# Attention products for two heads at once in a hybrid decoder layer, with a new order of the first stage

## The chip, the cores and the metric

One core of one Trainium2 chip. The metric is device time in microseconds (us) of one execution, the median of several runs. The kernel computes in float32; large products are made of three matmuls on halves of the numbers (below). Names: PE is the matmul engine TensorE, DVE VectorE, ACT ScalarE, POOL GpSimd, SP the engine that issues the DMAs.

## The reference

One decoder layer over 512 tokens of width 1024: native sparse attention (8 heads of 64, two groups of four heads that share keys and values) and a gated DeltaNet (4 heads of 128) in parallel, merged by gates, a layer norm, then a gated MLP with a short convolution (width 2816) and a second layer norm. What matters here:

```
# attention: three branches, each head's result weighted by a gate
p = jax.nn.softmax(s, axis=-1)              # s: scores of a branch, masked, with ALiBi
o = g[0] * o_cmp + g[1] * o_slc + g[2] * o_win      # o_x = p_x @ v_x
...
def conv_ffn(x, w_up, conv_w, w_down):
    h = causal_dwconv(x @ w_up, conv_w)     # width 3
    gate, val = jnp.split(h, 2, axis=-1)
    return (jax.nn.silu(gate) * val) @ w_down
```

With 512 tokens and 8 blocks of 64, the top 8 blocks are all blocks, so the selected branch and the window branch are causal attention over the whole sequence, with keys of their own.

## The kernel before

Every float32 matrix is split into a rounded part and the rest (names ending in h and l, or hi and lo; type F32R), and a product is hi·hi + hi·lo + lo·hi: three matmuls. ACT makes the hi part, DVE (sometimes POOL) the lo part. For weights these are the tiles `wh`, `wl` (`dh`, `dl` in the down-projection), from a tile `raw` that a DMA brings.

**First stage** (up to about 324 us): input projections (`gemm_t`, PSUM tile `pg`), the DeltaNet (`gdn_...`, PSUM `pd`) and the attention (PSUM `pa` for scores and transposes, `po` for results). Its steps are recorded by name and engine, then issued in the order that two tables give: `DRAWN`, the order of the steps, and `GIVEN`, the order of single instructions (`t0P*3` is three PE instructions of step t0, `@k` picks the k-th). `PLACE` says which buffer of a ring each new tile takes, `ENGINE` which engine does an operation that could run on several.

Attention of a head h has six units (`UNITS`): u = 0 to 3 are the token blocks 2 and 3 of each of the two large branches, u = 4 and 5 the blocks 0 and 1 of both branches at once. `scores(h, u)` makes scores and softmax weights in a `big` tile; `flip(h, u, s)`, issued one unit later (LAG), transposes them with PE into `pa`, from where ACT writes the hi part (`pth`) and DVE the lo part (`ptl`). After every second unit PE multiplies by the values (`vcat`, whose 128 columns hold hi and lo of the values): for u = 1, 3 the later 256 tokens, four key blocks; for u = 5 the earlier 256, two key blocks of two branches. Each key block takes a matmul with `pth` and one with `ptl`, 256 columns wide, all into one bank `po`. The compressed branch (`vcb` with `pc`) adds two matmuls 512 wide and closes the head; then `ob` copies the lower half of `po` and DVE adds both halves into `oT`. `po` has one buffer.

**Middle**: merge of the two mixers (PSUM `px`, `pm`), output projection (`pw`), layer norm. Here and later a scheduler orders the instructions by priority in the order of the code.

**FFN**: 22 tiles p, each a gate and a value half (b = 0, 1; PSUM `pu`): product, three convolution taps (ACT, then DVE twice, into `fa`), tanh and two products (`fth`, the last one on POOL). The down-projection is one level of Strassen-like sums over pairs of tiles: `halves` splits activations 11, 12, 22 and the sum s2 into hi and lo; s1, s3, s4 are kept in `SUM` and split later; `weight_sums` makes the sums of weights (`traw`) and sends them to `tdn`. Seven products (`mul`) follow, into PSUM `pdna` and `pdnb`; `add` adds a finished bank to `x1`, `work` holds generators that give out one piece of other work after every two weight tiles.

Of the kernel before, what the change touches and what calls it, by code (L numbers as in the profile page):

```python
# [18 lines left out]
S = 512  # L19
# [50 lines left out]
def layout(a):  # L70
# [18 lines left out]
    for i in range(8):  # L89
# [35 lines left out]
DRAWN = "q0 k0 i0 q1 j0 m0 c n0 i1 v0 j1 p0 v1 a0 o0 b0 y0 a1 b1 m1 n1 i2 j2 a2 b2 o1 y1 m2 v2 q2 a3 n2 b3 o2 y2 q3 p1 g0 k1 a4 i3 j3 b4 g1 m3 a5 n3 b5 a6 v3 g2 o3 b6 g3 a7 g4 b7 y3 g5 g6".split()  # L125
GIVEN = """
t0S@2 t0S@1 t0V@2 t0A@1 t0P@6 t0V@3 t0P@7 t0V@1 t0P@8 t0P@9 t0P@10 t0S t0A t0P@3 t0P@4 t0P@11 t0V t0P*3 t0S*2 t0V*2
t0A t0V t0P t0P@15 t0P@16 t0P@21 t0P*4 t2S t2A t0P@22 t0P@23 t2S t2A t0P*3 t2P@6 t2V*2 t2S t2A@3 t2A t2V t2P@3 t2P@9
t2P t2P@10 t2P@11 t2P*6 t2P@18 t2P@15 t2P@21 t2P@19 t2P@22 t2P*2 t2V t2P t2P@20 t2P@23 t2P*2 t4S@1 t4A@2 t4V@2 t4S
t4A@1 t4V@1 t4A t4P@9 t4P@10 t4V t4P t4P@3 t4P*2 t4S t4A t4P@11 t4P@6 t4P@7 t4P@21 t4P@8 t4P@22 t4P t4P@12 t4P@13 t4V  # L130
t4P@18 t4P t4P@15 t4P@16 t4P@17 t4P@19 t4P@20 t4P*2 t6S t6A t6S*2 t6A@2 t6A t6P@9 t6P@3 t6P@6 t6P t6V@2 t6V@1 t6P@10
t6P@7 t6V t6A t6P@4 t6P t6P@11 t6V t6P@8 t6P@18 t6P@5 t6P@19 t6P@20 t6P*5 t6P@21 t6P*4 w20S uA@8 w20A w20V w20A uA@2
uA@11 cV@8 cV@10 uA@5 w20V zS@6 dV@2 q0P*12 dV@3 dA*2 dV@4 dV@5 dV@6 dV@7 dV@8 dV@9 dV@1 dV@10 dV@11 q0P*12 w18S
w18A@1 w18V@1 uA@6 uV@2 zS@2 w21S w18A w18V k0P*15 dV@12 dV@13 dV@14 dV@15 k0P*2 uA@4 uA@7 uA@3 uA w0S q0A@2 q0A*2
dV@16 k0P*4 dV@17 dV@18 w0A zV@1 k0P q0V@2 q0V@1 q0V k0P w16S w0A w0V@1 w0V k0P k0V*4 dV@19 cS@1 i0P*13 zS@5 w21A w21V
dV@20 k0A*2 w1S uA@9 cV i0P*4 w1G i0P*3 s01P k0V*2 s01P i0P*3 s00P i0P q1P w21A q1P*12 s00P uV w1V i0V*2 dV@21 dV@22
w21V i0V zS s01V s01A q1P*8 uV@3 q1P*3 uA@10 zS i0V i0A zV w17S w1G dV@23 w1V dV@24 uV s04P*2 q1A uA j0P uV dA j0P*3
dV@25 dV@26 dV@27 dV j0P*12 w16A q1A@2 w16G q1A q1V@1 q1V@2 w16A w16G j0P*5 w4S j0P*3 q1V j0A w17A m0G j0V cP*19 i0G
cP m0P j0V*2 cS@3 m1V m0G m0P m0A cS i0G cP*4 dP w17V i0P dP i0P w4V w4V@2 dP i0P w4V*2 cA dA i0P j0A j0V i0A cS i0A
# [24 lines left out]
s21V n1V q2P*2 n1V*3 s25P v2A n1P w23V w23G n1P*3 n1A n1P y0V*2 n1P*3 n1V f21P y0P*3 s23A f21P y0P f21P n1P*3 s25V n1P
y0V s25A q2P s30P q2P*3 s30P n1V s23V v2V s24V f21P w22V s23V s30V f21A n1P*4 n1A n1P n1V n1P*7 n1A n1V q2P*3 n1P*6
f21V n1P*2 s23A q2P*2 n1A n1V q2P n1P@38 n1P@39 n1P@40 n1P@41 n1P*4 n1A@7 n1A f23P w23V s25V s25A v2V*2 f20P f23P*2
w23G m3G f20P f15V n1P*3 n2G@1 n1P n1A q2P*2 s25V s25V@4 q2P o1P o1A f22P f20P m2P*4 m2A o1P q3P*2 q2P o1V o1P@3 o1V@2
s25V f20A i2P*2 f22P f23P i2P*2 f20V f22P j2V i2A@6 i2A@7 i2A i2A@8 o1P@4 o1A q3P q2P q3P*2 o1P@6 o1V@3 i2A@9 i2A*3
i2V i2G q3P*3 o1P@8 w24S o1V@5 s30A m2P q2P*2 o1P@9 i2V*2 m2V m2P m2V@2 m2V q3P*7 w11S f22A q3P f22V s30V j1V j1G s30V
f23A m2P w11A f23V o1A@3 q2A q2A@2 q2A*2 q2V@1 q2V w11V s33P o1P@11 o1V@6 m2P m2V q3P n2V m1G w11A w11V f21P*2 s30A  # L170
f21P*6 s35P*2 n2V*2 q3P*7 q3A@2 q3V@1 q3A@1 w24V@1 s35V s35A s31P*2 s31V i2V@8 q3A@3 y2P*6 w12S y2P q3A y2P*5 f23P*4
w24V f23P y2P*7 m2V s35V s35A w24G@1 o1P@13 f25P*4 o1V@8 f24P*2 q3V w24G o1P@10 o1A@4 n2G n2P n2A y2P*2 w13S n2P n2A
n2V*5 s33P s33V n2V y2P*2 g0P f23P*2 f25A y2P g0P*10 y2A y2V f24A f23P f24V s34P n2V w19A w19V n2V s32P g0P f25P s35V
f25V s35V@4 m2G k1P*4 n2V*4 zV n2V k1P*2 g0P n2V g0P*4 n2V v2A g0P*2 k1P*3 w19A f25P*3 s31A s31V*2 f25P*4 w19V s33A
v2V s33V n2V s33V s33A s35A@3 s32P s32V g0P*5 s32A g0A w12V f25P*2 s34P s34V*2 s34A k1P*8 o1P@5 f30P o1A f25A n2V*5
# [39 lines left out]
PLACE = {  # L215
    'pg': '010101001010101010011010101010010',
    'pd': (
        '1010001100110001110100101111000001111101010110111001011001111000001001000000110111011010100101100010'
        '11000111010001110101010100101011001010101010101'
    ),  # L220
    'pa': (
# [1216 lines left out]
```

## Time and profile before

| what | value |
|---|---|
| median of 3 runs | 820.7 us (820.41 to 820.8) |
| profiled execution | 821.42 us |
| its span, first to last instruction | 819.6 us |
| mean granted PE clock | 0.997 |
| idle of DVE before `wl` of the later stages, for ACT `wh` | 21.6 us in 27 places |
| POOL waiting for DVE's `fa` | 194.0 us in 20 places |

How to read it: the page gives busy time by engine; the busy table by stage gives the same between two times; the list of waits says which engine stood still for which result of which other engine. Line numbers L261 and L1044 are those of the helper that records or passes on each instruction, so a tile's name tells more than its line. PE's matmuls overlap: the duration shown for one is longer than its distance to the next, and only the distance is a cost. A wait of an engine that nobody waits for costs nothing.

### The profile page before, as it was taken

The numbers are of one execution on the slowest core, as the hardware profiler recorded it, in microseconds if no ns is written. First come the engines' busy times: TensorE is split into PE (matmuls) and PEld (weight loads), VectorE is DVE, ScalarE is ACT, GpSimd is POOL, SyncE is SP. The second block draws the span as 40 slices with busy tenths as digits, with TensorE's granted clock in tenths as the row PEclk, the third lists the DMA queues.
The fourth block names the chain that finished last, engine by engine and source line by source line (L and its number), as shares of the span: only waits on it lengthen the run. The fifth ranks groups of instructions, "written<-read, shape, count | busy, mean of one in ns | idle before, by whom it ended". The sixth has DMA issues, their size and how long they took to land.

```text
span 819.6 us, 12072 instructions
## 1 busy us (share of the span) xinstructions
PE 808.5 (99%) x4244; PEld 684.8 (84%) x4244; DVE 638.2 (78%) x1379; ACT 400.9 (49%) x915; POOL 147.6 (18%) x127
## 2 busy tenths in 40 slices
PE   9999999999999999999999999999999999999996
PEld 9888888888888888887888897888888888878885
DVE  5979888887788777675467548878898889898767
ACT  5444665666776674534342023444444444566530
POOL 0031314232244401212300002111111011100001
PEclk9999999999999999999999999999999999999998
DMA  7432211111120201354463207555556655676922
GB/s 239 128 120 83 63 41 52 52 53 52 33 72 27 78 26 53 116 166 134 149 232 103 77 10 233 191 192 179 184 196 204 206 205 182 187 235 196 339 82 102
DMA packets 40252, 108.06 MB, mean 132 GB/s; under 512 B 4608, under 2 KB 5760, under 8 KB 39936
## 3 DMA queue, kind: packets, MB, share of 16 engines
q1 hardware_dynamic: 40192, 107.30, 39.7%
q8 instruction: 33, 0.54, 0.3%
q14 instruction: 27, 0.22, 0.1%
HBM read 93.65 MB, written 13.63 MB: 131 GB/s over the span
## 4 chain that ended last, share of the span: by engine, by line
PE 85%; DVE 6%; DMA 3%; ACT 2%; issue 2%; POOL 1%; SPq 0%; DVEq 0%; ACTq 0%; POOLq 0%
PE pu L261 25%; PE pg L1044 20%; PE pd L1044 8%; PE pa L1044 6%; PE pdna L261 5%; PE pdnb L261 5%; PE pm L261 5%; PE pw L261 3%; PE px L261 3%; PE po L1044 3%; PE pg L261 2%; DVE fa L261 1%; DVE x L261 1%; DVE wl L261 1%; DMA raw<-tdn 1%
## 5 line engine op out<-in xcount | busy, mean ns | idle before, releaser
L261 PE MATMUL pu<-mh,wl 128*128 128x512 f32 (+1 forms) x384 | 142.7, 372 | 0.7 <-DVE wl L261 0.7
L261 PE MATMUL pu<-mh,wh 128*128 128x512 f32 (+1 forms) x384 | 142.7, 372 | 0.0
L261 PE MATMUL pu<-ml,wh 128*128 128x512 f32 (+1 forms) x384 | 142.6, 371 | 0.0
L261 ACT ACTIVATE wh<-raw 128x512 fp32r<-128x512 f32 (+1 forms) x112 | 71.7, 643 | 80.7 <-PE pu L261 54.0
L261 DVE TENSOR_TENSOR wl<-raw,wh 128x512 fp32r<-128x512 f32 (+1 forms) x108 | 87.7, 817 | 25.6 <-ACT wh L261 21.6
L1044 PE MATMUL pg<-xh,wl 128*128 128x512 f32 x248 | 99.0, 402 | 0.0
L1044 PE MATMUL pg<-xl,wh 128*128 128x512 f32 x248 | 98.9, 400 | 0.0
L1044 PE MATMUL pg<-xh,wh 128*128 128x512 f32 x248 | 97.4, 399 | 0.0
L261 PEld LDWEIGHTS pu<-mh,wl 128*128 128x128 f32 x384 | 72.3, 188 | 13.6 <-DVE wl L261 1.2
L261 PEld LDWEIGHTS pu<-ml,wh 128*128 128x128 f32 x384 | 72.3, 188 | 12.6
L261 PEld LDWEIGHTS pu<-mh,wh 128*128 128x128 f32 x384 | 72.3, 188 | 12.4
L261 DVE SCALAR_TENSOR_TENSOR fa<-pu,fcw,fa 128x511 f32<-128x511 f32 x88 | 65.6, 746 | 10.0 <-ACT fa L261 8.6
L261 POOL TENSOR_TENSOR fth<-fth,fa 128x512 f32<-128x512 f32 x22 | 32.6, 1483 | 211.5 <-DVE fa L261 194.0
L1044 ACT ACTIVATE big<-big,mn 128x256 f32<-128x256 f32 (+3 forms) x84 | 46.0, 553 | 23.9 <-DVE mn L1044 22.2
L1044 POOL TENSOR_TENSOR wl<-raw,wh 128x512 fp32r<-128x512 f32 x28 | 36.6, 1313 | 99.7 <-ACT wh L1044 58.9
L1044 PEld LDWEIGHTS pg<-xh,wl 128*128 128x128 f32 x248 | 46.6, 188 | 9.5 <-issue 0.5
L1044 PEld LDWEIGHTS pg<-xl,wh 128*128 128x128 f32 x248 | 46.6, 188 | 9.0 <-issue 0.2
L1044 PEld LDWEIGHTS pg<-xh,wh 128*128 128x128 f32 x248 | 46.7, 188 | 8.7 <-issue 0.7
L261 ACT ACTIVATE dh<-raw 128x512 fp32r<-128x512 f32 x62 | 36.9, 624 | 23.9 <-DMA raw<-tdn 9.9
L261 DVE TENSOR_TENSOR dl<-raw,dh 128x512 fp32r<-128x512 f32 x62 | 41.1, 695 | 8.9 <-ACT dh L261 8.7
L1044 ACT ACTIVATE wh<-raw 128x512 fp32r<-128x512 f32 (+1 forms) x54 | 32.5, 607 | 9.1 <-PE pg L1044 5.0
L261 POOL TENSOR_TENSOR rs<-rs,minus_half 128x1 f32<-128x1 f32 x8 | 7.5, 942 | 163.2 <-DVE rs L261 163.2
(318 smaller groups left out, 1868.2 us busy)
## 6 DMA issues: line engine op xcount, KB each, us to landing
raw<-in_up SPq DMA_DIRECT2D x44, 512.0 KB, 4.0
raw<-in_wT SPq DMA_DIRECT2D x40, 512.0 KB, 3.5
traw<-in_down SPq DMA_DIRECT2D x22, 512.0 KB, 5.2
tdn<-traw SPq DMA_DIRECT2D x44, 256.0 KB, 2.7
raw<-tdn SPq DMA_DIRECT2D x20, 512.0 KB, 4.4
raw<-in_down SPq DMA_DIRECT2D x15, 512.0 KB, 4.0
raw<-in_wm SPq DMA_DIRECT2D x8, 512.0 KB, 3.6
raw<-in_wo SPq DMA_DIRECT2D x8, 512.0 KB, 3.5
```

Of the source, the lines that this page charges most:

```text
L261: return give(*a, **kw)
L1044: give(*a, **kw)
```

## The change

1. `flip` takes heads in pairs. `pth` and `ptl` (with slots for every branch and block, one part zeroed) are replaced by a ring `pt` of two tiles, hi and lo, that hold two heads, two blocks of 128 tokens (or two branches) and four key blocks. A step a0 to a11 now covers one pair of heads and two units each: four scores and four flips, then the products. Each product covers both heads: 512 columns, or 256 for the last key block, which only the later of the two token blocks can see. The later 256 tokens of a pair gather in one `po` tile over two steps, the earlier 256 in the next one. The compressed branch has four matmuls 256 wide per `po` tile, and `oT` is added per head in pieces of 256 columns.
2. `DRAWN`, `GIVEN` and `PLACE` are new tables, so every instruction of the first stage, the DMAs too, may stand elsewhere. `ENGINE` stays.
3. In the FFN, s2 (with its split) and s4 of a pair of tiles are issued in the next tile, after the taps of its gate half; the weight sums are then ordered behind the split of 22.
4. In the down-projection, six additions of the first product's banks are given out one by one during the second product.

```
-DRAWN = "q0 k0 i0 q1 j0 m0 c n0 i1 v0 j1 p0 v1 a0 o0 b0 y0 a1 b1 m1 n1 ...
+DRAWN = "q0 k0 i0 q1 j0 m0 c n0 i1 v0 j1 p0 v1 o0 a0 y0 a1 a2 m1 n1 ...
...
-BUFS = {... 'pc': 2, 'raw': 3, ...}
+BUFS = {... 'pc': 2, 'pt': 2, 'raw': 3, ...}
...
-    pth = nsa.tile([128, 2, 8, 128], F32R, name="pth")
-    ptl = nsa.tile([128, 2, 8, 128], F32R, name="ptl")
-    for t in (pth, ptl):
-        G.memset(t[:, :, 6, :].bitcast(F32), 0.0)
...
-        first = t - 2 if t > 1 else 4 + t
-        own = (slice(br, br + len(parts)), slice(first, first + 2 * t + 1, 2))
-        th, tl = pth[:, own[0], own[1], :], ptl[:, own[0], own[1], :]
+        pr, hh, e = h // 2, h % 2, u // 2
+        if (pr, e) not in PT:
+            PT[pr, e] = [R["pt"].tile((128, 2, 2, 4, 128), F32R) for _ in range(2)]
+        view = (lambda x: x[:, hh, :, t:3 * t + 1:2, :]) if t < 2 else (
+            lambda x: x[:, hh].rearrange("p b k c -> p (b k) c")[:, None, t - 2:3 * t - 1:2, :])
+        th, tl = (view(x) for x in PT[pr, e])
         A.activation(th, pt, AF.Copy)
         V.tensor_tensor(tl, pt, th.bitcast(F32), op=OP.subtract)
-        if t % 2 == 0:
+        if t % 2 == 0 or hh == 0:
             return
-        if u == 1:
-            POUT[h] = R["po"].tile()
-        pout = POUT[h]
+        late = t > 1
+        if e != 1:
+            POUT[late] = R["po"].tile((128, 2, 256))
+        pout = POUT[late]
+        split = [x.rearrange("p h b k c -> p h (b k c)") for x in PT.pop((pr, e))]
         for br, _ in parts:
-            for k in range(4 if t > 1 else 2):
-                o = pout[:, 256:] if t > 1 else pout[:, :256]
-                b = 2 * k if t > 1 else 4 + 2 * k
+            for k in range(t + 1):
                 w = vcat[:, k, br, g].rearrange("p a b -> p (a b)")
-                for i, src in enumerate((pth, ptl)):
-                    PE.matmul(o, w, src[:, br, b:b + 2, :], start=(u == 1 and k == 0 and i == 0), stop=False)
-        if u < 5:
+                a, z = (128 if k == t else 0), 256 * k + (0 if late else 512 * br)
+                for i, src in enumerate(split):
+                    PE.matmul(pout[:, :, a:], w, src[:, :, z + a:z + 256],
+                              start=(e != 1 and br == 0 and k == 0 and i == 0), stop=False)
+        if e == 0:
             return
-        j = h % 4
+        ts = slice(256, 512) if late else slice(0, 256)
         for i in range(2):
-            PE.matmul(pout, vcb[:, g, j].rearrange("p a b -> p (a b)"), PC[g][i], start=False, stop=(i == 1))
+            for n, pc in enumerate(PC[g]):
+                PE.matmul(pout[:, i], vcb[:, g, (h - 1 + i) % 4].rearrange("p a b -> p (a b)"), pc[:, ts],
+                          start=False, stop=(i == n == 1))
...
+        for i in range(2):
+            V.tensor_tensor(oT[pr][64 * i:64 * i + 64, ts], pout[0:64, i], ob[0:64, i], op=OP.add)
...
+    def second_sums(b, even, odd, after=None):
+        s2 = fs.tile([128, 256], F32, name="s2", bufs=1)
+        x = E("s2", b).tensor_tensor(s2, SUM["s1"][:, b], even, op=OP.subtract)
+        if after and E("s2", b) is V:
+            later(x, after)
+        halves("s2", b, s2)
+        E("s4", b).tensor_tensor(SUM["s4"][:, b], odd, s2, op=OP.subtract)
+
     for p in range(NF):
         g = []
         for b in range(2):
+            if b and p and p % 2 == 0:
+                second_sums(*held, turn)
...
-            s2 = fs.tile([128, 256], F32, name="s2", bufs=1)
-            E("s2", b).tensor_tensor(s2, SUM["s1"][:, b], ths[0][:, t1], op=OP.subtract)
-            done = halves("s2", b, s2)
-            E("s4", b).tensor_tensor(SUM["s4"][:, b], th[:, t1], s2, op=OP.subtract)
+            held = b, ths[0][:, t1], th[:, t1]
...
+    second_sums(*held)
...
-    for i in range(2):
-        add(i, n2, pa_[i], True)
-        add(2 + i, n1, pa_[i], True)
-        add(2 + i, n2, pa_[i], True)
+    def spread():
+        for i in range(2):
+            for t, cs in ((i, n2), (2 + i, n1), (2 + i, n2)):
+                yield add(t, cs, pa_[i], True)
+
+    work.append(spread())
     mul("s2", tdn[1], pb_)
+    work.clear()
```

What this does to the engines' queues, at three places. **PE, end of a head's products before, and end of the later tokens of a pair after** (the fourth pair of heads has the same form as each other pair; `po` is the result, `pc` the compressed branch's weights):

```order
L1044 MATMUL po_182<-pth,vcat 128x256
L1044 MATMUL po_182<-ptl,vcat 128x256
L1044 MATMUL po_182<-pc_154,vcb 128x512
L1044 MATMUL pg_184<-xl,wh_159 128x512
L1044 MATMUL po_182<-pc_155,vcb 128x512
```

```order
L1047 MATMUL po_184<-pt_156,vcat 128x512
L1047 MATMUL po_184<-pt_157,vcat 128x512
L1047 MATMUL po_184<-pt_156,vcat 128x2x128
L1047 MATMUL po_184<-pt_157,vcat 128x2x128
L1047 MATMUL po_184<-pc_154,vcb 128x256
L1047 MATMUL po_184<-pc_155,vcb 128x256
```

The products with `vcat` are now twice as wide or of two runs of 128, those with `vcb` half as wide.

**DVE, the first pair of FFN tiles and the start of the third tile** (`s` of two numbers is s1, then s2, then s4; `ls` and `hs` the halves of s2; `wl` the weights' low half, which PE waits for):

```order
L261 TENSOR_TENSOR s_4508<-fth 128x256
L261 SCALAR_TENSOR_TENSOR fa_4599<-pu_4574,fcw,fa_4599 128x511
L261 TENSOR_TENSOR s_4564<-s_4508,fth 128x256
L261 SCALAR_TENSOR_TENSOR fa_4599<-pu_4574,fcw,fa_4599 128x510
L261 TENSOR_TENSOR ls_4504<-s_4564,hs_4503 128x256
L261 TENSOR_TENSOR s_4510<-fth,s_4564 128x256
L261 TENSOR_TENSOR wl_164<-raw_157,wh_161 128x512
```

```order
L261 TENSOR_TENSOR s_4434<-fth 128x256
L261 SCALAR_TENSOR_TENSOR fa_4520<-pu_4495,fcw,fa_4520 128x511
L261 TENSOR_TENSOR wl_166<-raw_159,wh_162 128x512
L261 SCALAR_TENSOR_TENSOR fa_4520<-pu_4495,fcw,fa_4520 128x510
L261 TENSOR_TENSOR s_4524<-s_4434,fth 128x256
L261 TENSOR_TENSOR wl_164<-raw_159,wh_163 128x512
L261 TENSOR_TENSOR ls_4430<-s_4524,hs_4429 128x256
L261 TENSOR_TENSOR s_4436<-fth,s_4524 128x256
```

The first `wl` of the third tile stood behind s2, its split and s4, and now stands ahead of all three; the second stands between them.

**DVE, the second product of the down-projection** (`x` is the sum that `add` makes, `dl` the low half of the next weights):

```order
L261 TENSOR_TENSOR l_4498<-s_4509,h_4497 128x512
L261 SCALAR_TENSOR_TENSOR x_3928<-x_3928,pdna_6271 128x512 x3
L261 SCALAR_TENSOR_TENSOR x_3928<-x_3928,pdna_6272 128x512 x3
L261 TENSOR_TENSOR dl<-raw_158,dh 128x512 x2
L261 TENSOR_TENSOR dl<-raw_156,dh 128x512 x2
```

```order
L261 TENSOR_TENSOR l_4424<-s_4435,h_4423 128x512
L261 SCALAR_TENSOR_TENSOR x_3854<-x_3854,pdna_6197 128x512 x2
L261 TENSOR_TENSOR dl<-raw_158,dh 128x512 x2
L261 SCALAR_TENSOR_TENSOR x_3854<-x_3854,pdna_6197 128x512
L261 TENSOR_TENSOR dl<-raw_160,dh 128x512 x2
L261 SCALAR_TENSOR_TENSOR x_3854<-x_3854,pdna_6198 128x512
```

Six additions stood in a row; now two stand there, and the rest one by one between pairs of `dl`.

More of the change, by code (lines that the diff above doesn't have):

```diff
@@ L124 @@
 LAG = 1
[L125 removed]
+DRAWN = "q0 k0 i0 q1 j0 m0 c n0 i1 v0 j1 p0 v1 o0 a0 y0 a1 a2 m1 n1 i2 j2 a3 o1 y1 m2 v2 q2 a4 n2 a5 o2 y2 q3 p1 g0 k1 i3 j3 a6 g1 m3 a7 n3 a8 v3 g2 o3 a9 g3 a10 g4 a11 y3 g5 g6".split()
 GIVEN = """
[L127 removed]
@@ L215 @@
+BUFS = {'big': 23, 'rnd': 7, 'kq': 2, 'lx': 1, 'sq': 7, 'ts': 6, 'row': 16, 'mn': 3, 'k': 2, 'pc': 2, 'pt': 2, 'raw': 3, 'wh': 3, 'wl': 3, 'pg': 2, 'pd': 2, 'pa': 3, 'po': 1, 'mg': 6, 'mr': 4, 'dw': 7}
 PLACE = {
-    'pg': '010101001010101010011010101010010',
+    'pg': '010101001010101010011010101001101',
     'pd': (
-        '1010001100110001110100101111000001111101010110111001011001111000001001000000110111011010100101100010'
-        '11000111010001110101010100101011001010101010101'
+        '0101010101010110010011100010001011111000010001100100110110111111111000011110010011011001001000000001'
+        '11111001010011001011010111010100010101001111011'
@@ L230 @@
-    'wh': '0120212012102101201201120120120120121020122001210210210210212102101201012',
-    'wl': '0120212012101202102102210210212021010210200112021021021021202012101201012',
-    'rnd': '1023465451052164',
+        '0123456789afjcgi6b0k1m2349gik0465kc33a72g78626140jfdlhf8ge4a0lbk75jih7d1c0faf64f94l4dkijegcg6igf2ch4'
+        'f5mhlbh79dfc1ebl83ii3i94bj613llfecd04d4977f5ia317jbe0f9h37ii1ehfe1adk95561ah60gf71j80d69k59eg'
+    ),
+    'wh': '0120121021021021021012202120120120021012011220102101202102012020212100201',
@@ L233 @@
+    'wl': '0120120120210210210221102120120120210210211002120102101201021010120112012',
+    'rnd': '1045233623123046',
     'k': '0101',
     'kq': '0101',
-    'row': '0123579abf486cde1805437296cb',
-    'ts': '102431024153',
+    'row': '01234678b09a5cdef139467a2cd5',
+    'ts': '123405312540',
     'lx': '0000',
     'pc': '0101',
-    'mn': '101022210102120012122110122021010012001012012120',
+    'sq': '01231456426253410622503514301622154364465034212433165240',
+    'mn': '000211021022100021112021100120020120210212100212',
@@ L348, in body @@
     R = {n: Places(sp.tile, n, BUFS[n], size) for n, size in (
-        ("big", 512), ("rnd", 512), ("kq", 1024), ("lx", 1024), ("sq", 128), ("ts", 64), ("row", 16), ("mn", 8), ("k", 1024), ("pc", 512))}
+        ("big", 512), ("rnd", 512), ("kq", 1024), ("lx", 1024), ("sq", 128), ("ts", 64), ("row", 16), ("mn", 8), ("k", 1024), ("pc", 512), ("pt", 2048))}
     R.update({n: Places(wp.tile, n, BUFS[n], size) for n, size in (("raw", 1024), ("wh", 512), ("wl", 512))})
@@ L1004, in flip @@
-        Q2.pop(h)
+            for n, pc in enumerate(PC[g]):
+                PE.matmul(pout[:, i], vcb[:, g, (h - 1 + i) % 4].rearrange("p a b -> p (a b)"), pc[:, ts],
+                          start=False, stop=(i == n == 1))
+        ob = R["big"].tile((128, 2, 256))
+        copy(E("ob", 2 * pr + late, "A"), ob[0:64], pout[64:128])
+        if late:
+            oT[pr] = yo_tile("oT")
+        for i in range(2):
+            V.tensor_tensor(oT[pr][64 * i:64 * i + 64, ts], pout[0:64, i], ob[0:64, i], op=OP.add)
@@ L1029, in body @@
             continue
-        for u in (0, 1, 2) if name[0] == "a" else (3, 4, 5):
-            draw(f"s{at[0]}{u}", lambda: SC.append((at[0], u, scores(at[0], u))))
-            for x in SC[:] if u == 5 else SC[:-LAG]:
+        pr, e = divmod(at[0], 3)
+        for h, u in itertools.product((2 * pr, 2 * pr + 1), (2 * e, 2 * e + 1)):
+            draw(f"s{h}{u}", lambda: SC.append((h, u, scores(h, u))))
+            for x in SC[:] if h % 2 and u % 2 else SC[:-LAG]:
                 draw(f"f{x[0]}{x[1]}", flip, *SC.pop(0))
@@ L1206, in body, with later @@
     tr = pool(tq, name="tr", bufs=1, side="left")
+    def later(x, y):
+        tc.add_manual_dep(x.ins, y.ins.name, mybir.DependencyInfo(
+            mybir.DependencyClass.NoSync, mybir.DependencyReason.SCHED_ONLY), reason="not before its turn")
     def weight_sums(b, after):
@@ L1215, in weight_sums @@
         if e is V:
-            tc.add_manual_dep(one.ins, after.ins.name, mybir.DependencyInfo(
-                mybir.DependencyClass.NoSync, mybir.DependencyReason.SCHED_ONLY), reason="not before its turn")
+            later(one, after)
         e.tensor_tensor(b12, b22, b12, op=OP.subtract)
```

191 lines of the change are left out of this document (91 added, 100 removed).

## The prediction

> **What bounds the kernel now.** I read the page's busy times first, then busy times by stage, then the list of what TensorE (PE) waited for, and last the timelines of the places the change touches.
>
> ```profile
> PE 808.5 (99%) x4244; PEld 684.8 (84%) x4244; DVE 638.2 (78%) x1379; ACT 400.9 (49%) x915; POOL 147.6 (18%) x127
> ```
>
> ```profile
> 100.00:324.30 224.30, 223.88 (x1421) 193.74 (x1420) 183.15 (x572) 143.17 (x413) 67.12 (x60) 1.00 0.17 51
> 500.00:700.00 200.00, 199.74 (x881) 165.43 (x882) 174.27 (x281) 91.09 (x165) 25.63 (x19) 1.00 0.58 196
> ```
>
> The second fence is the busy table: length of the stage, then PE, PEld, VectorE (DVE), ScalarE (ACT), POOL, granted clock, DMA share, GB/s. 100 to 324 us is the stage with the attention, 500 to 700 the FFN's up-projection. PE is busy in practically all of both; DVE is second (82% and 87%). A busy PE could still be a PE that is spaced out, so I look at what it waited for (total us, times, longest):
>
> ```profile
> PE pg L261 <- DVE still L261: 1.0, 1, 1.0
> PE pu L261 <- DVE wl L261: 0.7, 1, 0.7
> PE pd L1044 <- ACT big L1044: 0.7, 1, 0.7
> PE pdnb L261 <- DVE dl L261: 0.5, 1, 0.5
> PE pd L1044 <- DVE big L1044: 0.3, 1, 0.3
> ```
>
> These five are nearly all of it (the others are 0.3 or less each). So a PE instruction that goes shortens the kernel by its spacing, and a wait that goes by its length; work on other engines counts only when it makes PE wait.
>
> **Part 1: products with the softmax weights for two heads.** Before, a head has 24 products 256 wide (vcat) and 2 products 512 wide (vcb): 192 and 16 in all. After, a pair of heads has 16 products 512 wide, 8 products 128 wide for each of two heads (256 columns; the last key block meets only the later half of the tokens), and 8 vcb products 256 wide: 64, 32 and 32. That is 80 instructions and 8192 columns less. Their price is the distance from start to start, not the duration shown:
>
> ```profile
> L1044 PE MATMUL po<-pth,vcat x96: 277/282/467, 100.9 to 322.4; 128*128 128x256 f32 x96
> 318.74 0.28 PE L1044 MATMUL po<-ptl,vcat 128*128 128x256 f32 x1
> ...
> 319.57 0.40 PE L1044 MATMUL pg<-xh,wl 128*128 128x512 f32 x1
> ```
>
> ```profile
> 128.59 0.40 PE L1044 MATMUL po<-pc,vcb 128*128 128x512 f32 x1
> 128.83 0.38 PE L1044 MATMUL pd<-sq,big 128*128 128x128 f32 x2
> ```
>
> ```profile
> 379.39 5.44 PE px L261 x24
> ```
>
> Seven products 256 wide take 319.57 - 318.74 = 0.83 us, so 0.119 each. One of 512 takes 0.24 beside other work (second fence) and 5.44/24 = 0.227 in a run (the chain of waits). Before: 192 x 0.119 + 16 x 0.24 = 26.7 us. After: 64 x 0.119 = 7.6, and 64 x 0.227 = 14.5 or 64 x 0.24 = 15.4: 22.1 to 23.0. The gain is 3.7 to 4.6 us; I take 4.1, since half of the new products stand in runs.
>
> The new 2x128 form writes two separated runs of a PSUM bank. The scores of the two short units do that already:
>
> ```profile
> 305.61 0.40 PE L1044 MATMUL pa<-k,rnd 128*128 128x256 f32 x2
> 305.84 0.40 PE L1044 MATMUL pg<-xh,wl 128*128 128x512 f32 x1
> ```
>
> Two in 0.23 us, 0.115 each: no dearer than a contiguous one. The Trainium skill says otherwise ("PSUM — Partial Sum Buffer", Specifications (TRN2)): any non-contiguous access pattern slows matmuls significantly. This row speaks against it; what it would cost is a rival below.
>
> Another rule bears on the size. The Trainium skill ("TensorE: Matmul & The Clock Gate", Back-to-back issue gap) gives about 81 ns sustained for a matmul 128 wide and 131 for 512, so the count would weigh more than the columns. Estimated from that page along a straight line (98 ns for 256), Part 1 would gain 6.2 us. The 0.227 above disagrees.
>
> Beside PE, 8 additions into oT become 16 of half the width, and reading PSUM they cost
>
> ```profile
> L1044 DVE TENSOR_TENSOR oT<-po,big 64x512 f32<-64x512 f32 x8 | 5.4, 678 | 0.1
> L1044 DVE TENSOR_TENSOR big<-pd,big 128x256 f32<-128x256 f32 x12 | 4.7, 415 | 0.2 <-ACT pth L1044 0.2
> ```
>
> 5.4 us before and about 16 x 0.415 = 6.6 after: 1.2 more on DVE, which has 224.3 - 183.2 = 41 us free in this stage. I cost it at nothing; without that cover it is at most 1.2. Two POOL memsets go, on an engine busy 67 of 224 us: nothing.
>
> **Part 2: the first stage's order.** All engines' instructions, and SP's DMA issues with them, stand in a new order. Old waits of PE in this stage (up to 324 us) are 0.7 and 0.3 in the list above, plus 1.0 at the start, which is the memset and stays. The new order can win at most 1.0. It can lose as much by a transfer or a split that now comes late; PE's list names no DMA, so the loads have slack. I take 0, and keep -1.0 and +1.5.
>
> **Part 3: sums of the activations.** Place of the first wait (PE, then DVE):
>
> ```profile
> 499.14 0.39 PE L261 MATMUL pu<-ml,wh 128*128 128x512 f32 x1
> 500.26 0.50 PE L261 MATMUL pu<-mh,wl 128*128 128x512 f32 x1 [0.73 <-DVE wl L261]
> 500.60 0.39 PE L261 MATMUL pu<-mh,wh 128*128 128x512 f32 x1
> ```
>
> ```profile
> 497.20 0.75 DVE L261 SCALAR_TENSOR_TENSOR fa<-pu,fcw,fa 128x511 f32<-128x511 f32 x1 [0.31 <-ACT fa L261]
> 497.86 0.41 DVE L261 TENSOR_TENSOR s<-s,fth 128x256 f32<-128x256 f32 x1
> 498.20 0.74 DVE L261 SCALAR_TENSOR_TENSOR fa<-pu,fcw,fa 128x510 f32<-128x510 f32 x1
> 498.86 0.41 DVE L261 TENSOR_TENSOR ls<-s,hs 128x256 fp32r<-128x256 f32 x1
> 499.19 0.42 DVE L261 TENSOR_TENSOR s<-fth,s 128x256 f32<-128x256 f32 x1
> 499.52 0.68 DVE L261 TENSOR_TENSOR wl<-raw,wh 128x512 fp32r<-128x512 f32 x1
> ```
>
> PE stands 500.26 - 499.14 = 1.12 us where 0.227 is due, and the next gap is 0.34: (1.12 - 0.23) + (0.34 - 0.23) = 1.0 us lost. It wants the wl that DVE starts at 499.52, behind s2, a tap, ls and s4. The new order has wl right behind the first tap, so it can start at 497.86 and end near 498.5, before PE's 499.37. The stall goes: 1.0 us. Next late is the following wl, behind s2; PE wants it 12 matmuls (2.7 us) on, about 502.1, and it can be ready near 500. In the ten later pairs there is nothing to win (PE busy 199.74 of 200) and DVE has 26 of 200 us free. The new wait is ACT's tanh on s2, which reads the fth buffer that tanh overwrites; behind it on ACT stand the next wh splits. But s2 stands next to the second tap, for which tanh waits anyway: at most 0.4 us a pair, 4 us if nothing covered it. PE has wl buffers ahead; I take 0. The last pair's sums stay where they were.
>
> **Part 4: six additions in the down-projection** (PE, DVE, ACT):
>
> ```profile
> 727.06 0.39 PE L261 MATMUL pdnb<-dh,hs 128*128 128x512 f32 x1
> 728.00 0.50 PE L261 MATMUL pdnb<-dl,hs 128*128 128x512 f32 x1 [0.55 <-DVE dl L261]
> 728.33 0.39 PE L261 MATMUL pdnb<-dh,ls 128*128 128x512 f32 x1
> ```
>
> ```profile
> 723.67 3.67 DVE L261 SCALAR_TENSOR_TENSOR x<-x,pdna 128x512 f32<-128x512 f32 x6
> 727.26 3.69 DVE L261 TENSOR_TENSOR dl<-raw,dh 128x512 fp32r<-128x512 f32 x6
> ```
>
> ```profile
> 722.92 1.15 ACT L261 ACTIVATE dh<-raw 128x512 fp32r<-128x512 f32 x2
> ```
>
> PE loses (0.94 - 0.23) + (0.33 - 0.23) = 0.8 us for a dl whose dh was ready at 724.07 but which stood behind six additions of 0.61. With two ahead of it, dl starts at 723.67 + 1.2 = 724.9 and is done by 725.5: the stall goes, 0.8 us. What the additions release, the pdna banks, is wanted by the next product (DVE, then the chain of waits):
>
> ```profile
> 731.27 0.69 DVE L261 TENSOR_TENSOR dl<-raw,dh 128x512 fp32r<-128x512 f32 x1
> ```
>
> ```profile
> 737.59 14.96 PE pdna L261 x66
> ```
>
> The sixth addition stands right behind this dl, the last of its product, so it ends by about 732.6, 5 us before PE asks. Nothing lost; without that cover, one addition, 0.6.
>
> **The sum** is made on the profiled execution, 821.42 us (span 819.6, and 1.8 around it): 4.1 + 0 + 1.0 + 0.8 = 5.9, so 815.5. That execution lay 0.7 above the median of 820.7, so as a median 814.8.
>
> **The rivals.**
> - *Slower: the pair's buffers become a chain.* All twelve sets of four flips write the same two pt tiles, and no flip of the next set may be split until the last product of this one has read them; before, units had slots of their own. The rows:
>
> ```profile
> L1044 ACT ACTIVATE pth<-pa x48: 362/560/662, 76.4 to 319.7; 128x512 fp32r<-128x512 f32 x24, 128x384 fp32r<-128x384 f32 x16, 128x256 fp32r<-128x256 f32 x8
> L1044 DVE TENSOR_TENSOR ptl<-pa,pth x48: 408/613/692, 83.9 to 320.3; 128x512 fp32r<-128x512 f32 x24, 128x384 fp32r<-128x384 f32 x16, 128x256 fp32r<-128x256 f32 x8
>   PE po L1044: 2.8, 4
> ```
>
> ACT waited on products even before (2.8 us in 4 places). Four splits of 0.56 and a last one on DVE of 0.61 are 2.9 us in which PE needs other work, at 11 joints. Against it: the new order has at least 12 projection matmuls (2.7 us) and the transposes and scores of the flips between any two sets. It decides when 5.9/11 = 0.54 us a joint stay uncovered; at 1.0 us a joint the time is 814.8 + 11 = 825.8.
> - *Products shorter, but PE waits in their place.* DVE, at 82%, cannot follow the faster stage; only parts 3 and 4 remain: 820.7 - 1.8 = 818.9. Against it: 41 us of free DVE time, PE's waits of 1.0.
> - *The FFN waits move one buffer on* instead of going: 820.7 - 4.1 = 816.6.
> - *The new order also removes the old waits* and the products run at 0.227: 820.7 - 4.6 - 1.0 - 1.8 = 813.3.
> - *Two-run writes at double spacing:* 32 x 0.119 = 3.8 back, 818.6. (This is the PSUM page's rule, named above.)
> - *Products paid by count:* if a 512 cost little more than a 256, 26.7 us shrink by the share of instructions, 128 of 208: 16.4, 10.3 less, 808.6. The 0.227 against 0.119 speaks against it. (The TensorE page of the Trainium skill leans this way.)
>
> **How the numbers follow.** Forecast 0.60; FFN waits move 0.13; waits removed too 0.10; waits in place 0.08; chain 0.05; two-run writes 0.03; by count 0.01. The likeliest gives 814.8. Bounds of parts 1 and 2 make 814.8 - 1.5 = 813.3 to 814.8 + 1.9 = 816.7; to leave out no more than 2 in 10 I go down to 812.8 and up to 818.6. A change within 0.2% (1.6 us) is about what a measurement of this kernel cannot tell from none: 819.1 to 822.3. Below 819.1 lie the forecast, the moved waits, the removed waits, two-run writes, count, and half of the waits in place: 0.90. Same: 0.05 (the rest of those and a mild chain). Slower: 0.05.
>
> **What would show it.** po products: 64 at 512, spacing 0.227 to 0.24, 64 at 256, spacing 0.119, the sum near 22.5 us; no wait of pu for wl near the first FFN tiles; none of pdnb for dl; PE's other waits before 320 us under 2 us. I am wrong if PE's list shows po waiting for pt splits, if 2x128 products are spaced wider than 0.12, or if wl waits appear between 500 and 700 us.

## The result, and the profile after

| kernel | median us | runs | lowest to highest |
|---|---|---|---|
| before | 820.7 | 6 | 819.81 to 820.97 |
| changed | 814.9 | 6 | 814.27 to 815.43 |

The ratio is 0.9928, 95% interval 0.9918 to 0.9938: 5.9 us less. The profiled execution of the changed kernel took 815.05 us, with a span of 813.0. Lines moved by three: L1047 is now the helper that passes on the first stage's instructions (L1044 before).

The page's busy times, then the busy table of the attention's stage and of the FFN's up-projection (length, PE, PEld, DVE, ACT, POOL, clock, DMA share, GB/s):

```profile
PE 803.6 (99%) x4164; PEld 679.5 (84%) x4164; DVE 636.9 (78%) x1387; ACT 398.5 (49%) x915; POOL 146.6 (18%) x125
```

```profile
100.00:320.30 220.30, 219.12 (x1345) 187.10 (x1344) 185.06 (x584) 146.97 (x432) 67.99 (x59) 1.00 0.16 49
500.00:700.00 200.00, 200.00 (x884) 165.58 (x884) 174.95 (x282) 91.88 (x169) 24.79 (x19) 1.00 0.58 196
```

PE has 80 instructions less and is still busy in practically all of both stages; DVE's work there has hardly changed (183.2 us before), but the first stage around it is shorter. What PE waited for in the changed kernel, the whole list:

```profile
PE pg L261 <- DVE still L261: 1.0, 1, 1.0
PE pd L1047 <- DVE big L1047: 0.7, 2, 0.5
PE pg L1047 <- DVE rnd L1047: 0.3, 1, 0.3
PE pd L1047 <- ACT wh L1047: 0.2, 1, 0.2
```

The memset's 1.0 at the start stands. `pu<-wl` and `pdnb<-dl` are gone, and so is `pd<-ACT big`; `pd<-DVE big` is partly new.

**Where the time went.** I take the start of the first matmul that writes a tile as the border of a stage:

| stage, from the first matmul of ... to that of ... | before | changed | difference |
|---|---|---|---|
| start to `px` (first stage) | 324.16 | 320.31 | -3.85 |
| `px` to `pm` | 16.33 | 16.34 | 0 |
| `pm` to `pw` (merge) | 76.81 | 76.16 | -0.65 |
| `pw` to `pu` | 46.81 | 46.53 | -0.28 |
| `pu` to `pdna` (FFN up) | 242.55 | 241.52 | -1.03 |
| `pdna` to the last matmul (FFN down) | 105.68 | 104.83 | -0.85 |
| from there to the end | 7.30 | 7.30 | 0 |

That is 6.6 us between two single executions, against 5.9 between the medians. The merge's 0.65 is a wait that the profiled execution of before happened to have:

```profile
370.69 0.39 PE L261 MATMUL px<-xl,wh 128*128 128x512 f32 x1
371.39 0.50 PE L261 MATMUL px<-xh,wl 128*128 128x512 f32 x1 [0.31 <-DVE wl L261]
371.73 0.40 PE L261 MATMUL px<-xh,wh 128*128 128x512 f32 x1
```

The first experiment below has before's first stage and merge, and its merge takes 76.16 too (`pw` to `pu`: 46.41). So these two pieces are no effect of the change.

**The products** in the changed kernel: two groups by count, and the last set in PE's order of time.

```profile
L1047 PE MATMUL po<-pt,vcat x96: 274/389/582, 116.8 to 317.9; 128*128 128x512 f32 x64, 128*128 128x256 f32 x32
...
L1047 PE MATMUL po<-pc,vcb x32: 277/280/385, 147.1 to 318.4; 128*128 128x256 f32 x32
```

```profile
316.19 0.85 PE L1047 MATMUL po<-pt,vcat 128*128 128x512 f32 x4
316.87 0.40 PE L1047 MATMUL pg<-xl,wh 128*128 128x512 f32 x1
```

The row of four stands for two of 512 and two of the two-run form (merged rows carry the first one's shape). They take 316.87 - 316.19 = 0.68 us: 2 x 0.227 + 2 x 0.113. Over the whole trace, from the start of each `po` product to the start of the matmul behind it, the old 208 products sum to 27.66 us and the new 128 to 23.11: 4.55 less. The stage gained 3.85, so in this execution the new order gave 0.7 back.

**The place of the FFN stall** (PE, then DVE), some 5 us earlier than it was:

```profile
494.14 0.39 PE L261 MATMUL pu<-mh,wh 128*128 128x512 f32 x1
494.37 0.39 PE L261 MATMUL pu<-ml,wh 128*128 128x512 f32 x1
494.60 0.39 PE L261 MATMUL pu<-mh,wl 128*128 128x512 f32 x1
```

```profile
492.44 0.75 DVE L261 SCALAR_TENSOR_TENSOR fa<-pu,fcw,fa 128x511 f32<-128x511 f32 x1 [0.31 <-ACT fa L261]
493.11 0.68 DVE L261 TENSOR_TENSOR wl<-raw,wh 128x512 fp32r<-128x512 f32 x1
493.71 0.74 DVE L261 SCALAR_TENSOR_TENSOR fa<-pu,fcw,fa 128x510 f32<-128x510 f32 x1
494.37 0.42 DVE L261 TENSOR_TENSOR s<-s,fth 128x256 f32<-128x256 f32 x1
494.70 0.69 DVE L261 TENSOR_TENSOR wl<-raw,wh 128x512 fp32r<-128x512 f32 x1
```

`wl` stands directly behind the first tap, ends at 493.79, and PE reads it at 494.60 with no gap. The next `wl`, behind s2, ends at 495.39; PE wants it 12 matmuls later.

**The place of the down-projection's stall** (PE, then DVE):

```profile
721.26 0.39 PE L261 MATMUL pdnb<-dh,hs 128*128 128x512 f32 x1
721.49 0.39 PE L261 MATMUL pdnb<-dl,hs 128*128 128x512 f32 x1
721.72 0.39 PE L261 MATMUL pdnb<-dh,ls 128*128 128x512 f32 x1
```

```profile
718.12 1.28 DVE L261 SCALAR_TENSOR_TENSOR x<-x,pdna 128x512 f32<-128x512 f32 x2
719.32 1.29 DVE L261 TENSOR_TENSOR dl<-raw,dh 128x512 fp32r<-128x512 f32 x2
720.52 0.68 DVE L261 SCALAR_TENSOR_TENSOR x<-x,pdna 128x512 f32<-128x512 f32 x1
721.12 1.29 DVE L261 TENSOR_TENSOR dl<-raw,dh 128x512 fp32r<-128x512 f32 x2
```

The row of six additions has become two, then one ahead of each later pair of `dl`. PE keeps its 0.23.

**The new wait** stands at the end of the first stage (PE, DVE, POOL):

```profile
318.51 0.49 PE L1047 MATMUL pd<-ident,big 128*128 128x128 f32 x3
319.48 0.77 PE L1047 MATMUL pd<-ident,big 128*128 128x128 f32 x5 [0.48 <-DVE big L1047]
```

```profile
317.42 0.16 DVE L1047 TENSOR_TENSOR row<-row 128x4 f32<-128x4 f32 x1 [0.56 <-POOL row L1047]
317.61 1.81 DVE L1047 TENSOR_TENSOR big<-big,row 128x512 f32<-128x512 f32 x1
```

```profile
316.38 1.01 POOL L1047 TENSOR_TENSOR row<-row,minus_half 128x4 f32<-128x4 f32 x1 [6.55 <-DVE row L1047]
317.58 1.29 POOL L261 TENSOR_TENSOR wl<-raw,wh 128x512 fp32r<-128x512 f32 x1 [0.20 <-DVE row L1047]
```

Third of eight transposes to the fourth: 318.73 to 319.48, 0.75 where 0.11 is due, 0.64 lost. The fourth waits for a tile that DVE scales in 1.81 us; other such rows take 0.69. POOL had started a split 0.03 us before. Some 8 us earlier POOL delays the same sort of row in another way (DVE, then POOL):

```profile
309.86 0.16 DVE L1047 TENSOR_TENSOR row<-row 128x4 f32<-128x4 f32 x1 [1.35 <-POOL row L1047]
```

```profile
307.56 1.29 POOL L261 TENSOR_TENSOR wl<-raw,wh 128x512 fp32r<-128x512 f32 x1 [2.92 <-PE pg L1047]
308.81 1.02 POOL L1047 TENSOR_TENSOR row<-row,minus_half 128x4 f32<-128x4 f32 x1
```

Its other split of that weight stands ahead of a power that DVE needs, and DVE idles 1.35 us.

### The profile page after: what moved, and what is told of

It is laid out like the page before. It is cut to its first block, busy times and chain, and to the rows that moved or that the text cites. A ratio compares the mean times of both kernels' runs of the same rounds, so it can differ in the third digit from the quotient of the medians.

```text
span 813.0 us, 11879 instructions
## 1 busy us (share of the span) xinstructions
PE 803.6 (99%) x4164; PEld 679.5 (84%) x4164; DVE 636.9 (78%) x1387; ACT 398.5 (49%) x915; POOL 146.6 (18%) x125
## 4 chain that ended last, share of the span: by engine, by line
PE 75%; DVE 3%; ACT 1%; POOL 0%; issue 0%; DVEq 0%; ACTq 0%
PE pu L261 30%; PE pg L1047 7%; PE pdna L261 7%; PE pdnb L261 6%; PE pw L261 5%; PE pm L261 5%; PE px L261 3%; PE pd L1047 3%; PE pa L1047 3%; PE pg L261 3%; PE po L1047 1%; DVE big L1047 1%; ACT big L1047 1%; PE pt L261 0%; DVE x L261 0%
## 5 line engine op out<-in xcount | busy, mean ns | idle before, releaser
L1047 PE MATMUL pg<-xh,wh 128*128 128x512 f32 x248 | 98.7, 402 | 0.3 <-DVE rnd L1047 0.3
L1047 PE MATMUL pg<-xl,wh 128*128 128x512 f32 x248 | 98.7, 400 | 0.0
L1047 PE MATMUL pg<-xh,wl 128*128 128x512 f32 x248 | 98.3, 398 | 0.0
L1047 PEld LDWEIGHTS pg<-xh,wh 128*128 128x128 f32 x248 | 46.6, 188 | 9.7 <-DVE rnd L1047 0.7
L1047 PEld LDWEIGHTS pg<-xl,wh 128*128 128x128 f32 x248 | 46.7, 188 | 8.5 <-issue 0.2
L1047 PEld LDWEIGHTS pg<-xh,wl 128*128 128x128 f32 x248 | 46.6, 188 | 8.6
L1047 ACT ACTIVATE big<-big,mn 128x128 f32<-128x128 f32 (+3 forms) x84 | 45.6, 552 | 13.8 <-DVE mn L1047 13.0
L1047 POOL TENSOR_TENSOR wl<-raw,wh 128x512 fp32r<-128x512 f32 x28 | 36.3, 1306 | 82.8 <-ACT wh L1047 34.8
L1047 ACT ACTIVATE wh<-raw 128x512 fp32r<-128x512 f32 (+1 forms) x54 | 32.6, 609 | 16.2 <-PE pg L1047 8.9
```

The costliest lines, as they stand in the source:

```text
L1047: give(*a, **kw)
```

## Experiments

All are measured beside runs of the kernel before on the same chip; ratios are to those, with 95% intervals. Before's median was 820.9 in the first group and 821.4 in the others.

### The two FFN parts, and the attention's, each alone

The kernel before with the diff's parts 3 and 4:

```diff
--- before
+            if b and p and p % 2 == 0:
+                second_sums(*held, turn)
...
+    work.append(spread())
     mul("s2", tdn[1], pb_)
+    work.clear()
```

> The kernel before with parts 3 and 4 alone (the late activation sums and the six additions given out). My theory: the two stalls go, 1.0 + 0.8 = 1.8 us, whatever the attention does: 820.7 - 1.8 = 818.9, and the lists of waits show neither pu<-wl near 500 us nor pdnb<-dl near 728 us. Rival, the waits move one buffer on: 820.7, with a new wait of about the same length one split later. Rival, they win only together with the new attention: also 820.7.

Measured: 819.0 us, ratio 0.9978 (0.9969 to 0.9988), 1.9 less. PE's list:

```profile
PE pd L1044 <- ACT xh L1044: 1.3, 1, 1.3
PE pg L261 <- DVE still L261: 1.0, 1, 1.0
PE pd L1044 <- ACT big L1044: 0.7, 1, 0.7
PE pd L1044 <- DVE big L1044: 0.3, 1, 0.3
```

Neither FFN wait is there. The wait for `xh`, at about 7 us, stands among the first products and is no effect of the edit: it differs by a microsecond or more between executions of the same instructions (0.2 in the profiled execution of before). It leaves this execution 0.55 us late at 10 us, and 0.55 still at 66 us.

The changed kernel with both undone:

```diff
--- changed
-    work.append(spread())
+    for i in range(2):
+        add(i, n2, pa_[i], True)
+        add(2 + i, n1, pa_[i], True)
+        add(2 + i, n2, pa_[i], True)
     mul("s2", tdn[1], pb_)
...
-            held = b, ths[0][:, t1], th[:, t1]
+            s2 = fs.tile([128, 256], F32, name="s2", bufs=1)
+            E("s2", b).tensor_tensor(s2, SUM["s1"][:, b], ths[0][:, t1], op=OP.subtract)
+            done = halves("s2", b, s2)
+            E("s4", b).tensor_tensor(SUM["s4"][:, b], th[:, t1], s2, op=OP.subtract)
```

> The changed kernel with parts 3 and 4 undone: parts 1 and 2 alone. My theory: the products are worth 4.1 and the order nothing, 820.7 - 4.1 = 816.6, and the two old stalls are back (0.7 and 0.5 in the list of waits). Rival, VectorE cannot follow the shorter first stage: 818.9 or more. If it comes out under 816 the FFN parts are worth less than 1.2 in the changed kernel.

Measured: 816.7 us, ratio 0.9948 (0.9934 to 0.9961), 4.2 less. Both stalls are back (PE):

```profile
493.95 0.39 PE L261 MATMUL pu<-ml,wh 128*128 128x512 f32 x1
495.07 0.50 PE L261 MATMUL pu<-mh,wl 128*128 128x512 f32 x1 [0.73 <-DVE wl L261]
...
721.87 0.39 PE L261 MATMUL pdnb<-dh,hs 128*128 128x512 f32 x1
722.71 0.50 PE L261 MATMUL pdnb<-dl,hs 128*128 128x512 f32 x1 [0.45 <-DVE dl L261]
```

Its up-projection takes 242.55 us from border to border and its down-projection 105.58: 1.03 and 0.75 more than in the changed kernel, so that is what each part is worth. 4.2 + 1.9 = 6.1 against 5.9 together: the halves add up, and the waits didn't move on.

### Columns, count, order, or the two-run form?

First the old width and count in the new order (`both` issues a list of products as one step of it, so that the order stays):

```diff
--- changed
                 for i, src in enumerate(split):
-                    PE.matmul(pout[:, :, a:], w, src[:, :, z + a:z + 256],
-                              start=(e != 1 and br == 0 and k == 0 and i == 0), stop=False)
+                    first = e != 1 and br == 0 and k == 0 and i == 0
+                    z0 = z - (256 if a else 0)
+                    halves = [(pout[:, n], w, src[:, n, z0:z0 + 256]) for n in range(2)]
+                    steps[into[-1]].setdefault("P", []).append((both, (halves, first), {}))
```

> The changed kernel, order and all, with its 96 vcat products issued in the old width and count: every 512 as two of 256, and each two-run 256 as two full 256 (the last key block's products use the weights of the block before it, so that part of the output is another sum). 192 of 256 columns instead of 64 of 512 and 32 of 256. By spacing (0.119 for 256, 0.238 for 512 beside other work): 192 x 0.119 - 64 x 0.238 - 32 x 0.119 = +3.8 us, 814.9 + 3.8 = 818.7. Rival, the new order is what won the time: 814.9. Rival, products are paid by count: 96 more of 0.119 = +11.4, 826.3.

Measured: 818.1 us, ratio 0.9964 (0.9951 to 0.9976). Then the same columns as in the changed kernel, with 64 instructions more:

```diff
--- changed
                 for i, src in enumerate(split):
+                    first = e != 1 and br == 0 and k == 0 and i == 0
+                    if a:
+                        PE.matmul(pout[:, :, a:], w, src[:, :, z + a:z + 256], start=first, stop=False)
+                        continue
+                    halves = [(pout[:, n], w, src[:, n, z:z + 256]) for n in range(2)]
+                    steps[into[-1]].setdefault("P", []).append((both, (halves, first), {}))
```

> The changed kernel with each 512 wide vcat product issued as two of 256, same columns, 64 instructions more. By columns: 64 x (2 x 0.119 - 0.230) = +0.5 us, 815.4. By count: 64 x 0.119 = +7.6, 822.5. With the run above it says how much of the gain is columns left out (the last key block) and how much is the count.

Measured: 814.7 us, ratio 0.9926 (0.9914 to 0.9939). The two differ by 818.11 - 814.66 = 3.45 us: 32 instructions of 256, 8192 columns (3.8 by the spacing). So most of the gain of parts 1 and 2, 3.45 of 4.2, is **the columns left out**, the last key block's for the earlier half of the tokens, and not the smaller count. By medians the 64 instructions that only split a 512 cost nothing (814.7 against 814.9), but the traces show that two things cancel there: the changed kernel's profiled execution has the new wait of 0.64 us and this one's hasn't, while the products' distances sum to 23.77 us against 23.11. That is 0.66 for 64 instructions, 0.01 each, near the 0.5 expected. Against the old widths (27.29) the products' sum differs by 3.52, of which the 32 instructions as such would make 0.3 at that price. The rest is left open: the old widths in the new order lie 0.9 below the FFN parts alone (818.1 against 819.0), of which the products themselves make 0.4 (27.29 us against 27.65).

The two-run form, issued as one run:

```diff
--- changed
+                    if a:
+                        PE.matmul(pout[:, i], w, src[:, i, z - 256:z], start=first, stop=False)
+                    else:
+                        PE.matmul(pout, w, src[:, :, z:z + 256], start=first, stop=False)
```

> The changed kernel with each of its 32 two-run products (2x128, in two separated halves of the bank) issued as one contiguous 256 of one head (same count and columns; it reads another block's weights, so that part of the output is another sum). My theory: a two-run write costs what a contiguous one does, 0.119: 814.9. Rival, separated runs cost double: 32 x 0.119 = 3.8 us less, 811.1.

Measured: 814.3 us, ratio 0.9912 (0.9898 to 0.9926), against 0.9928 (0.9918 to 0.9938) for the changed kernel. The products' sum over the trace is 23.09 us against 23.11, and the 32 alone take 4.01 us in both. Two runs cost what one does.

### The new wait, taken out

```diff
--- changed
-'wh31': 'V',
+'wh31': 'V', 'ws31': 'V',
```

In the table of engines this gives VectorE both `wl` splits of that merge weight, which POOL does in the changed kernel.

> The changed kernel, but the two wl splits of one merge weight (POOL at 317.58 us and its neighbour) are done by VectorE. My theory of the new wait at 318.7 us (0.64 us of PE): VectorE's 512 wide product of two SBUF tiles took 1.81 instead of 0.69 because it started beside that POOL split and ended 0.55 after it; without POOL there it takes 0.69, ends about 318.9 at the latest and the wait goes: 0.5 to 0.6 us less than the changed kernel, 814.3. Rival, the instruction is long for another reason (ScalarE and PE at the same place): 1.8 stays and the time is 814.9. Rival, VectorE's two more splits of 0.69 delay something else: 814.9 to 815.5.

Measured: 813.3 us, ratio 0.9902 (0.9888 to 0.9916). The place in the new trace (DVE, then PE):

```profile
317.07 0.69 DVE L1047 TENSOR_TENSOR big<-big,row 128x512 f32<-128x512 f32 x1
317.68 0.69 DVE L261 TENSOR_TENSOR wl<-raw,wh 128x512 fp32r<-128x512 f32 x1
```

```profile
317.96 1.03 PE L1047 MATMUL pd<-ident,big 128*128 128x128 f32 x8
318.75 0.48 PE L1047 MATMUL pg<-xh,wl 128*128 128x512 f32 x1
```

The scaling takes 0.69, and eight transposes run in 0.79. That is more than was expected: the small stalls behind the other split, 0.24 and 0.18 at 311 us, went too. Since even before's median differs by 0.5 us between the groups, the next two runs stand beside each other on one chip: the changed kernel again, and the mended one.

> The changed kernel as it is, beside the two below, so that they are compared on one chip: 814.9 again.

> The changed kernel with the two wl splits on VectorE once more, now beside the changed kernel. From the two traces: the wait at 318.7 us (0.64 us) and the two short ones at 310.9 and 311.4 us (0.24 + 0.18) are gone, 1.1 us in all: 813.8. Rival, the 1.5 between the two calls was the chip's and not the kernel's: within 0.3 of the changed kernel.

Measured: the changed kernel 814.4 (0.9918, 0.9904 to 0.9931), the mended one 813.3 (0.9901, 0.9887 to 0.9915). The intervals to before overlap a little; all four timed runs of the mended kernel (812.91 to 813.7) lie below all four of the changed one (814.23 to 815.79), 1.1 between the medians. The version with this one entry more beats both kernels.

But the 1.1 did not come as expected. In the second profiled execution of the changed kernel the wait at 318.7 was missing, though the program is the same (DVE, then POOL):

```profile
317.74 0.69 DVE L1047 TENSOR_TENSOR big<-big,row 128x512 f32<-128x512 f32 x1
```

```profile
317.74 1.83 POOL L261 TENSOR_TENSOR wl<-raw,wh 128x512 fp32r<-128x512 f32 x1 [0.23 <-DVE row L1047]
```

Here the two start in the same hundredth, DVE wins, and POOL pays: 1.83 instead of 1.29. Of the six profiled executions that have POOL's split at this place (this kernel's two, and the attention's parts alone, the old widths, the split 512 and the one run), POOL started first in two, and VectorE took 1.81 both times; in the other four VectorE started first and took 0.69. So what the two traces of the pair show of the 1.1 is 0.71 in the first stage (319.77 against 319.06 us), all of it lost at 311 us; the rest is not shown, and that the expected number came out is partly luck.

### How much the softmax split's chain can bear

ScalarE's split of the softmax weights, twice in a row:

```diff
--- changed
-        A.activation(th, pt, AF.Copy)
+        def twice():
+            nc.scalar.activation(th, pt, AF.Copy)
+            nc.scalar.activation(th, pt, AF.Copy)
+
+        steps[into[-1]].setdefault("A", []).append((twice, (), {}))
```

> The changed kernel with ScalarE's half of every softmax weight split (pt<-pa, 48 of them, about 0.56 us each) issued twice in a row: the chain of a pair's set (split, subtract, product, next split) becomes about 4 x 0.56 = 2.2 us longer at each of the 11 joints, 27 us more of ScalarE in all. My theory: PE stands behind no pt today, and the joints have 2.7 us of other work each; up to 2 us is lost, most of it where ScalarE is late for something else: 815 to 817. Rival, the chain is just covered: all of it shows, 11 x 2.2 = 24 us, 839, with PE's list naming po <- pt.

Measured: 825.6 us, ratio 1.0049 (1.0035 to 1.0063): 10 to 11 us more than the changed kernel, between the two theories and expected by neither. So the same time goes on ScalarE where neither the subtraction nor a product waits for it (nothing reads the tile `spare`):

```diff
--- changed
+        def and_more():
+            nc.scalar.activation(th, pt, AF.Copy)
+            for i in range(2):
+                nc.scalar.activation(spare, C["alibi"][:, 176 * i:176 * i + 176], AF.Copy)
+
+        steps[into[-1]].setdefault("A", []).append((and_more, (), {}))
```

> The changed kernel with ScalarE copying 2 x 176 columns of a constant into a spare tile right behind each of the 48 pt splits, some 0.6 us more of ScalarE each, as much as the second split of the run before, but neither the subtraction nor the pa bank nor the pt tile waits for it. If what that run lost (10.7 us) went by ScalarE's queue, being late for everything behind, most of it is lost here too: 822 or more. If it went by the chain split - subtract - product - next split, which is 0.56 longer there and as before here: under 3 us, 815 to 818.

Measured: 823.5 us, ratio 1.0027 (1.0018 to 1.0037), 9.1 more than the changed kernel beside it (814.4). The page of this run, and what PE waited for most:

```profile
PE 806.1 (98%) x4164; PEld 677.7 (82%) x4164; DVE 636.3 (77%) x1387; ACT 424.4 (52%) x1011; POOL 146.1 (18%) x125
```

```profile
PE pd L1054 <- DVE big L1054: 3.2, 3, 1.3
PE pa L1054 <- DVE pt L1054: 1.3, 2, 0.7
```

So most of the loss needs no longer split: 25.9 us more of ScalarE (424.4 - 398.5), spread over the stage, make what stands behind in its queue late, and PE loses 9.1. With the splits twice in a row it is 2.1 us more (825.6 against 823.5), and PE's list names there what it doesn't name in this run or in the changed kernel:

```profile
PE po L1052 <- ACT pt L981: 1.3, 2, 0.7
PE po L1052 <- DVE pt L1052: 0.6, 3, 0.2
```

Those are products that wait for the pair's splits, 1.9 us in 5 places. They need not be the whole price of the chain: in the run with the copies, 14 of the 48 splits start directly behind a copy, so sets of splits are longer there too, and weight loads of the products wait for `pt` in both (4.7 us in 9 places with the split twice, 2.0 in 5 with the copies, 0.3 in one in the changed kernel). The two runs don't separate the chain from the queue. The buffers of the pair bind no more than they did. ScalarE's wait for the products, in the view of tile `pt`, is in the changed kernel

```profile
  PE po L1047: 3.3, 2
```

and in both of these runs 3.0 in two places. Four `pt` buffers in place of two weren't tried.

## Why the prediction was right, step by step

- **What bounds.** PE, in both stages shown. The sum of its gone columns and gone waits gave the result; the time was 814.9 where 814.8 stood. That it fits within 0.1 is partly luck: in the profiled executions the products gave 0.45 more than the 4.1 put down and the order 0.7 less than its 0. And in the last group of runs the changed kernel lay 7.0 below before (814.4 against 821.4), not 5.9.
- **Part 1**, put at 4.1 (3.7 to 4.6). Parts 1 and 2 alone measured 4.2. In the trace the products went from 27.66 to 23.11, 4.55, at the upper end: the old ones cost 1.0 more than their spacing says, which I put down to those that stand beside other work (not shown), and the new ones took 23.11 where 22.1 to 23.0 was worked out. That 0.119 for 256 and 0.227 for 512 is close to a price by columns is shown by the split and the old widths: 8192 columns and 32 instructions made 3.5 us, 64 instructions without columns 0.66.
- **Part 2**, put at 0 (-1.0 to +1.5). In the profiled execution it lost 0.7: old waits went (`pd<-ACT big` 0.7 among them), and new ones came, 0.64 and 0.42, at a place that the prediction doesn't name, where POOL's two splits meet VectorE's scaling. In the second profiled execution, without the 0.64, the first stage ends at 319.77 us, and only 0.16 of the products' 4.55 is lost. By medians the new order with the old widths in it came out 0.5 better than the old one, beyond the products' own 0.4. What the order is worth by itself stays open between these two. All of it lies inside the bounds, but the reasoning "PE's list names no DMA, so the loads have slack" left out that two engines can meet in a new place. The 0.64 comes and goes between executions.
- **Part 3**, put at 1.0: 1.03 by the borders, with `wl` ending at 493.79, earlier than PE wants it by 0.8 us, and the next one in time. No later pair has a wait.
- **Part 4**, put at 0.8: 0.75 to 0.85. The six additions lie as described, and no product waits for the banks.
- **The rivals.** Slower by the pair's buffers: ScalarE's wait on products went from 2.8 us in 4 places to 3.3 in 2, and none of PE's waits is for `pt`. The cover that the prediction claims for the joints holds with the splits as they are; with splits twice as long, 2.2 us more at each of 11 joints, PE's products waited 1.9 us for them in all, the sign that the prediction names. Waits in place of the products, waits moved on, and two-run writes at double spacing each had an experiment, and none of them showed; of payment by count 0.66 us showed for 64 instructions, where the count alone would have made 7.6. "The new order also removes old waits" is half there: old ones went, others came.
- **DVE's 1.2 us more at no cost.** DVE's busy time fell in sum (638.2 to 636.9), and no wait of PE is for `oT`. But the ScalarE run shows that "the engine has time to spare" is a weak reason: ScalarE too had 73 us to spare in this stage (220.3 - 147.0), and 25.9 us of work cost 9.1.
- **What I didn't forecast** are the merge's 0.65 and the 0.28 behind it. The merge's wait stood in before's list at 0.3, among those that the prediction passed over. They belong to the one execution of before that was profiled, and that execution's 0.7 above the median is of this size.

## What to carry to other kernels

Where PE is the bound, price a change of its instructions by the columns they stream, take the spacing from a run of the same form in the trace, and look for columns that are multiplied for nothing, here a key block that half of the tokens can't see. A stall that shows as one wait of PE behind a queue of another engine is worth its length and can be had by moving what stands ahead in that queue, if the next thing it makes late has slack. Idle time of a second engine is no slack by itself: it is slack only where nothing in order behind the added work is wanted soon.

## What the runs showed of the hardware

**VectorE and POOL shut each other out where both read two SBUF tiles, and the first to start wins.** With POOL's split started 0.03 us earlier, VectorE's scaling of two SBUF tiles ran 1.81 us and ended 0.55 after POOL (317.58 + 1.29 = 318.87, 317.61 + 1.81 = 319.42). With both at 317.74, VectorE took its 0.69 and POOL 1.83, some 0.54 more than its 1.29. In the FFN the same happens beside POOL's product, where PE has other buffers and doesn't wait (DVE):

```profile
541.02 1.57 DVE L261 TENSOR_TENSOR wl<-raw,wh 128x512 fp32r<-128x512 f32 x1 [0.44 <-ACT wh L261]
```
The Trainium skill says just this ("SBUF — State Buffer", SBUF: two separate sides): the port pair that the two share is an exclusive lock, whichever starts first gets it for the whole instruction, and two SBUF inputs are enough for VectorE to need it against a POOL instruction that reads SBUF. The trace agrees, down to the loser: 0.03 us of start decide which of the two it is, and so whether PE loses 0.64 us in that execution.

**A matmul's count cost little here, its columns nearly all.** 64 instructions more with the same columns made the products' distances 0.66 us longer in sum, 0.01 each, against 0.113 to 0.119 for a matmul of 256 columns. A write in two runs of a PSUM bank cost what one run does: 32 of them took 4.01 us in both forms.
